# Half blocks, cast blocks and quarter stores of a two-level Winograd matmul on other queues and slots

## The chip, the cores and the metric

The kernel runs on one core of one Trainium2 chip. The metric is device time in microseconds (us) of one execution. Before the change it is 1529.64 us, the median of three runs (1527.75 to 1530.28). TensorE, VectorE, ScalarE and GpSimd work as separate engines; SyncE only issues transfers. In the lines of the profile they are PE (its weight loads PEld), DVE, ACT, POOL and SP. Transfers are issued by GpSimd (queue q0 of the page) and by SyncE (q1), and all of them run on the core's 16 DMA engines.

## The reference

```python
def setup_inputs():
    m, k, n = 4096, 4096, 4096
    return {"a": randn(m, k), "b": randn(k, n), "bias": randn(n)}   # float32

def reference(a, b, bias):
    return np.tanh(np.matmul(a, b) + bias)
```

## The kernel before

**Tiling.** The output is cut into four columns of 1024 (`c` = 0 to 3) and sixteen pairs of row blocks (256 rows). Of each pair and column the product is made by Winograd's variant of Strassen's scheme: the 256 x 4096 by 4096 x 1024 product is split into quadrants, and seven products of 16 matmuls of 128x128 by 128x512 (`m1` to `m7`, the table `PRODUCTS`) take the place of eight. Operands are fp16, sums float32. On the left stand the quadrants `a11`, `a12`, `a21`, `a22` and their sums `s1`, `s2`, `s5`, `s6`, `s7`; on the right `b11`, `b22` and the sums `d1`, `d3`, `d4`, `e6`, `e7`, each kept in four blocks (`b11_0` to `b11_3`). `b11_0` and `e6_0` are the two halves of one tile that is called `side`.

**Two pairs at once.** In columns 1, 2 and 3 most row pairs are taken by two (`fours`), and then most products are split a second time by the same scheme (`group0`, `group1`, `single`; 128x256 matmuls of line 764). For that `m2` and `m6` need forms of their right operand: quarters and the sums `t1`, `t2`, `t4`, `t3`. They are written to DRAM ahead of time by `put_four` and `put_sum`, and read back through a ring of five tiles (`b11_1`, `b11_2`, `b11_3`, `e6_2`, `e6_3`) by `pull_four`, each time that `let_go` frees one. So the blocks of `b11` and `e6` are overwritten while a column's fours run. Two halves that no form in DRAM holds are saved by `put_corner` and those of `m3`, `m4`, `m5` and `m7` that `t3` takes the place of are saved by `move(..., True)`.

**Leaving.** The last four of columns 1 and 2 (`leave` in `four`) must put the single blocks back, because the next row pairs use them whole. `give_back(c, step)` does that by the table `BACK`: `bring_block` reads a block back as two half blocks of 256 KB, `move(..., False)` returns the saved `t3` halves, `fetch` reads quadrants (`guest`), `load_nat` reads rows of `a` that must still be transposed, `load_raw` loads blocks of the next column's `b`. Steps 0 to 10 lie in the products of the four, 11 to 17 in the whole products `m1`, `m6`, `m7` at its end, 18 on in the slots behind. In the kernel before, `bring_block` uses GpSimd's queue at steps below `DIRECT` = 8 and SyncE's from there on; `move` always uses SyncE's. SyncE's queue carries the output stores, the quadrants and the writes of transposed rows too; each queue issues in program order, so a transfer that waits holds up those behind it.

**The leaving of column 1** ends with row pair 4; the next are pair 3 (item 25, its quadrants in DRAM already) and pair 2 (item 26), 0 and 1 (items 27, 28), whose rows are read in float32 and transposed by VectorE (`load_nat`, `turn`; line 237 for item 26, line 245 for 27 and 28). The second half of the four's last product `m7` is made between the first products of item 25. The rows of item 26 come at step 11 and just behind step 14; then, slot by slot (a slot is one product, 3.45 us), rows of 27 and 28 and blocks of column 2's `b` (`change`): `b12`, `b21`, then `b11`, `b22`, of which `bsum` makes `d3`, `e6`, `d1`, `d4`, `e7` on VectorE.

**Casting.** GpSimd's queue reads float32 blocks of `b` as four quarters of 128 KB, converted on the way. `cast_b` writes such a block of column 3 to DRAM in fp16, a quarter at each call, and `load_b` then reads it in one transfer. Before, this is done in the inner fours of column 2 (steps 0, 2, 6 and 9), for three whole blocks.

**Entering.** `begin_four` places the writes of forms around the start of the fours, in slots relative to `s0`, two items ahead: `ADDED` for `t3`, `STAGED` for `t1`, `t2`, `t4` (made on VectorE, so GpSimd's queue waits for it), `ASIDE` for the quarters, `SAVED` for the corners. From slot 8 on, `turn_over` carries out these slots itself (`slot(8)` and so on).

Of the kernel before, what the change touches and what calls it, by code (L numbers as in the profile page):

```python
# [44 lines left out]
SLOTS = 7  # L45
# [14 lines left out]
TWICE = (1, 2, 3)  # L60
# [3 lines left out]


FOUR = ((0, 0), "t1", (1, 0), "t2", "t3", (1, 1), "t4")
ADDED = {
# [3 lines left out]
}  # L71
STAGED = {1: (-8, -6, -4, 1, 4, 7), 2: (-8, -6, -4, 1, 4, 7), 3: (-8, -6, -4, 1, 4, 7)}
ASIDE = {1: (-7, -5, -3, 1, 3, 6), 2: (-7, -5, -3, 1, 3, 6), 3: (-12, -7, -10, -2, 6, 4)}
SAVED = {1: (-3, -2, 0, 2), 2: (-3, -2, 0, 2)}
SPARED = (0, 1)
S6_AT = 2
AWAY = {"m5": -14, "m7": -3}
# [7 lines left out]

CAST = [(3, blk, *half) for half in ((0, 1), (1, 0)) for blk in range(2)]
CASTING = {2: (0, 2, 6, 9)}


BACK = {
    1: {
        ("e6", 0): 6, ("e6", 1): 7, ("m7", "t3"): 7, ("guest", "a21"): 8, ("b11", 0): 9, ("b11", 1): 9, ("b11", 2): 10,
        ("b11", 3): 10, ("m5", "t3"): 9, ("m3", "t3"): 14, ("m4", "t3"): 15, ("nat", 1): 11, ("guest", "a12"): 10,
    },
# [4 lines left out]
    },  # L101
}
DIRECT = 8

OVER_FOUR = {"t3": (0, 1)}
HALF = (ds(0, NB // 2), ds(NB // 2, NB // 2))
# [14 lines left out]
def kernel(  # L121
# [7 lines left out]
    nc = tc.nc  # L129
# [53 lines left out]
    partner, begins, ends_with, firsts = {}, {}, {}, {}  # L183
# [33 lines left out]
    nat, aset = {}, {}  # L217
# [79 lines left out]
    def fetch(n, name, queue=nc.sync):  # L297
        for here, there in stored(n, name):
            queue.dma_start(out=here, in_=there)
# [53 lines left out]
    def cast_b(c, blk, h, j):  # L353

        to = dram.tile([P, TB, NB], fp16, name=f"cast_{c}_{blk}_{h}_{j}")
        for i in range(4):
            load_b(to, c, blk, h, j, quarters=(i,))
            if i == 3:
                cast[c, blk, h, j] = to
            yield  # L360
# [229 lines left out]
    def quarter(what, r, j, i):  # L590

        return bop[TWO[what][1], 2 * r + i][:, :, HALF[j]]
# [23 lines left out]
    def move(what, c, out_, *names):  # L616

        for name, (r, j) in OVER_FOUR.items():
            if names and name not in names:
                continue  # L620
            if out_:
                away[what, c, name] = dram.tile([P, TP, NB // 2], fp16, name=f"away_{what}_{c}_{name}")
            for i in range(2):
                there = away[what, c, name][:, ds(i * TB, TB)]
                here = quarter(what, r, j, i)
                nc.sync.dma_start(*(there, here) if out_ else (here, there))

    def twice_after(n, what):
        c, (pair,), part, _ = items[n]
# [53 lines left out]
    def bring_block(name, blk, queue=nc.gpsimd):  # L683
        what = {"b11": "m2", "e6": "m6"}[name]
        r, i = divmod(blk, 2)
        to = new_bop(name, blk)
        for j in range(2):
            there = corners[name, blk] if (r, j) == (0, 1) else forms[what, (r, j)][:, ds(i * TB, TB)]
            queue.dma_start(out=to[:, :, HALF[j]], in_=there)
# [162 lines left out]
    def give_back(c, step):  # L852
        for (name, part), at in BACK[c].items():
            if at == step:
                if name == "nat":
                    load_nat(ends_with[c] + 1, part)
                elif name == "guest":
                    fetch(ends_with[c], part)
                elif name in TWO:
                    move(name, c, False, part)  # L860
                elif name in ("b12", "b21"):
                    load_raw(name, c + 1, part, nc.sync)
                else:
                    bring_block(name, part, nc.gpsimd if step < DIRECT else nc.sync)

    left_over = []

    def four(n):
        c = items[n][0]
        p, q, m = n, n + 1, n + 2  # L870
        first, last = n == begins[c], m == len(items)
# [8 lines left out]
        def step(k):  # L880
            if leave:
                give_back(c, k)
            elif not first and not last and k in CASTING.get(c, ()):
                next(casts, None)

        def one_whole(what, i, steps=range(T)):
            _, left_, right = next(v for v in PRODUCTS.values() if v[0] == what)
# [221 lines left out]
        if last:  # L1109
# [15 lines left out]
            for what, (name, at, op, scale, r) in ends.items():  # L1125
                o, here = st[q][name], bank(q, 0, at)
# [44 lines left out]
    def begin_four(c):  # L1171
        s0 = SLOTS * (begins[c] - 2)
        n = next(n for n in firsts if firsts[n] == c)
        at_slot(SLOTS * n + 4, take_d, n)
        added = ADDED.get(c, {})
        for stage, slots in added.items():
            for add, at in enumerate(slots):
                at_slot(s0 + at, put_sum, *stage, add)
        for at, stage in zip(
            STAGED[c] + ASIDE[c],  # L1180
            [i for i in STAGES if i not in added] + [(w, f) for w in ("m2", "m6") for f in ((0, 0), (1, 0), (1, 1))],
        ):
            at_slot(s0 + at, put_four, *stage)
        for at, (name, blk) in zip(SAVED.get(c, ()), (("b11", 0), ("b11", 1), ("e6", 0), ("e6", 1))):
            at_slot(s0 + at, put_corner, name, blk)

    def turn_over(c):

        m = begins[c]
        p, q = m - 2, m - 1  # L1190
        left_count[0] = 0
        del free[:]

        def slot(at):
            for f, args in work.pop(SLOTS * p + at, ()):
                if f in (put_four, put_sum, put_corner):
                    f(*args)

        queue.extend(
            (what, f) for n in range(m, ends_with[c], 2) for what in ("m2", "m6")  # L1200
            for f in (FOUR if what == "m2" else (*FOUR[:5], *reversed(FOUR[5:])))
            if what == "m2" or n + 2 in fours or c == NC - 1
        )
        returned.clear()
        if c < NC - 1:
            returned.append(c)
        free.extend(("b11_1", "b11_2", "b11_3"))
        for i in range(3):
            pull_four()
        asum(q, "s1")  # L1210
        asum(q, "s6")
        fetch(m, "a11")
        slot(8)
        product(p, *PRODUCTS[8])
        single(p, "m4", 7)
        adds["m4"][1]()
        product(q, *PRODUCTS[2])
        resident_at(-7)
        single(p, "m4", 3)
        twice_after(p, "m4")  # L1220
        twice_four(p, "m4", 3)
        fetch(m, "a22")
        fetch(m + 1, "a22")
        fetch(m + 1, "a11")
        asum(q, "s7")
        slot(9)
        slot(10)
        seed(m, "d", 0)
        resident_at(-6)
        product(q, *PRODUCTS[5])  # L1230
        fetch(m, "a21")
        slot(12)
        resident_at(-5)
        slot(13)
        product(p, *PRODUCTS[10])
        resident_at(-4)
        seed(m, "w", 0)
        seed(m + 1, "w", 0)
        left(m, "m4", "v1")
        left(m, "m3", "v1")  # L1240
        slot(15)
        resident_at(-3)
        product(q, *PRODUCTS[8])
        fetch(m + 1, "a21")
        free.extend(("e6_2", "e6_3"))
        for i in range(2):
            pull_four()
        slot(17)
        resident_at(-2)
        seed(m, "c", 0)  # L1250
        product(q, *PRODUCTS[10])
        resident_at(-1)
# [50 lines left out]
    def at_slot(slot, f, *args):  # L1303
        work.setdefault(slot, []).append((f, args))
# [173 lines left out]
    first = new_sum([P, 4, 4, TB * QP], fp16, "first")  # L1478
    coarse = [bops.tile([P, 4, TB * QP], fp32, name="coarse", tag=t) for t in ("d3_1", "d3_2")]

    def load_first(m, queue, out_):
# [9 lines left out]
        out=ident, in_=ident, compare_op=mybir.AluOpType.is_equal, fill=0.0,  # L1491
# [146 lines left out]
    for c in TWICE:  # L1638
        s0 = SLOTS * next(n for n in range(len(items)) if items[n][0] == c)
        at_slot(s0 + 10, rights.clear)  # L1640
        at_slot(s0 + 10, new_right, "m4", "t1", "t2")
        if c == 2:
            at_slot(s0 + 10, new_right, "m4", "t4")
        at_slot(s0 + 10, new_right, "m3", "t1", "t2")
        at_slot(s0 + 12, new_right, "m3", "t4")
        if c != 2:
            at_slot(s0 + 14, new_right, "m4", "t4")
        for name, m3_at, m4_at in zip(("t1", "t2", "t4", "t3"), *FORMED):
            at_slot(s0 + m3_at, kept_form, "m3", name)
            at_slot(s0 + m4_at, kept_form, "m4", name)  # L1650
        at_slot(s0 + 14, new_lefts)
        if c < NC - 1:
            for what, there in (("m3", 6), ("m4", 10)):
                at_slot(s0 + there, move, what, c, True)
    for c in FOURS:
        begin_four(c)
    casts = (None for where in CAST for _ in cast_b(*where))
    groups = {}
    for n in partner:
        s0 = SLOTS * n  # L1660
# [15 lines left out]
    for slot in range(1 - len(ORDER), SLOTS * len(items)):  # L1676
        if slot in handed:
            if slot - 1 not in handed:
                c = max(c for c in FOURS if SLOTS * (begins[c] - 2) < slot)
# [50 lines left out]
```

## Time and the profile before

| What | before |
|---|---|
| median of three runs | 1529.64 us |
| the profiled execution | 1528.55 us |
| its span, first to last instruction | 1526.8 us |
| mean granted TensorE clock | 0.994 |
| bytes moved by DMA | 407.75 MB |
| transfers issued by GpSimd, share of 16 engines (q0) | 57.5% |
| transfers issued by SyncE (q1) | 36.6% |

Stretches are given in us from the span's start. In the table by stretches each engine has its busy time and in brackets its instructions; then come the granted TensorE clock (1.00 is full speed), the share of time that the packets of both queues together took on the 16 DMA engines (above 1 when packets of the two queues lie over each other), and GB/s. A line of the timeline has the start, the duration, the engine, the source line, the operation and its tiles, with the idle time of the engine before it and what ended it in square brackets. A line of an SP or POOL transfer there is its issue; when it landed is told by the table of DMA issues, whose last column is the median time from issue to landing.

### The profile page before, as it was taken

The numbers are of one execution on the slowest core, as the hardware profiler recorded it, in microseconds if no ns is written. First come the engines' busy times: TensorE is split into PE (matmuls) and PEld (weight loads), VectorE is DVE, ScalarE is ACT, GpSimd is POOL, SyncE is SP. The second block draws the span as 40 slices with busy tenths as digits, with TensorE's granted clock in tenths as the row PEclk, the third lists the DMA queues.
The fourth block names the chain that finished last, engine by engine and source line by source line (L and its number), as shares of the span: only waits on it lengthen the run. The fifth ranks groups of instructions, "written<-read, shape, count | busy, mean of one in ns | idle before, by whom it ended". The sixth has DMA issues, their size and how long they took to land.

```text
span 1526.8 us, 24983 instructions
## 1 busy us (share of the span) xinstructions
PE 1501.6 (98%) x9461; PEld 925.4 (61%) x9461; DVE 1214.9 (80%) x1718; ACT 403.4 (26%) x909; POOL 505.0 (33%) x894
## 2 busy tenths in 40 slices
PE   9999999999999999988999999999999999999998
PEld 4444444444445788853444578778744458888887
DVE  6788977777878888856788788789638869888888
ACT  4431111111222233320122223332212222333332
POOL 7765453433433111153553312222135121111112
PEclk9999999999999999998999999999999999999999
DMA  9999999999989788999997979999999687888895
GB/s 178 182 249 267 294 248 249 214 212 243 178 242 300 270 304 322 340 277 249 233 211 239 306 261 312 334 334 320 307 262 223 219 257 275 308 300 315 319 343 188
DMA packets 220269, 407.75 MB, mean 267 GB/s; under 512 B 25971, under 2 KB 114547, under 8 KB 220149
## 3 DMA queue, kind: packets, MB, share of 16 engines
q0 software_dynamic: 122320, 211.08, 57.5%
q1 hardware_dynamic: 97156, 194.68, 36.6%
q8 instruction: 74, 1.21, 0.3%
q10 hardware_dynamic: 672, 0.39, 0.1%
q14 instruction: 47, 0.38, 0.1%
HBM read 347.08 MB, written 133.69 MB: 315 GB/s over the span
## 4 chain that ended last, share of the span: by engine, by line
PE 86%; DMA 9%; DVE 2%; POOL 1%; issue 1%; SPq 0%; ACT 0%; DVEq 0%; POOLq 0%; ACTq 0%
PE ps L472 39%; PE ps L764 35%; PE ps L828 8%; PE ps L1414 4%; DMA nat<-in_a_dram 3%; DMA b<-in_b_dram 1%; DMA out_dram<-o 1%; DMA b<-form_m 1%; DMA out_dram<-ds 1%; DMA side<-in_b_dram 1%; DVE a L265 1%; DMA land<-in_a_dram 0%; POOL nat L228 0%; POOL land L1455 0%; DVE s L151 0%
## 5 line engine op out<-in xcount | busy, mean ns | idle before, releaser
L472 PEld LDWEIGHTS <-a 128*128 128x128 f16 x2592 | 254.0, 98 | 323.7 <-DMA b<-form_m 11.7
L764 PEld LDWEIGHTS <-h 128*128 128x128 f16 x2944 | 287.7, 98 | 37.4 <-DVE h L151 1.4
L700 POOL DMA_DIRECT2D form<-form_m x196 | 103.7, 530 | 551.6 <-PE ps L764 489.6
L764 PEld LDWEIGHTS <-a 128*128 128x128 f16 x2208 | 216.0, 98 | 36.2 <-issue 3.3
L472 PE MATMUL ps<-b,a 128*128 128x512 f16 x868 | 200.6, 382 | 11.6 <-DMA b<-form_m 10.3
L472 PE MATMUL ps<-d,a 128*128 128x512 f16 x800 | 182.2, 381 | 4.7 <-DVE ps L151 4.7
L265 DVE STREAM_TRANSPOSE a<-nat 128x1024 f16<-128x1024 f16 (+3 forms) x178 | 155.9, 918 | 18.4 <-PE ps L472 13.1
L375 POOL DMA_DIRECT2D b<-in_b_dram x240 | 129.5, 545 | 96.8 <-DMA b<-in_b_dram 30.1
L472 PE MATMUL ps<-e,a 128*128 128x512 f16 x700 | 159.2, 379 | 0.0
L151 DVE TENSOR_TENSOR a<-a,a 128x2048 f16<-128x2048 f16 (+1 forms) x123 | 148.2, 1205 | 0.2
L764 PE MATMUL ps<-form,h 128*128 128x256 f16 x1136 | 144.8, 273 | 0.1
L151 DVE TENSOR_TENSOR h<-a,h 128x1024 f16<-128x1024 f16 x184 | 125.1, 686 | 16.0 <-PE ps L764 15.6
L472 PEld LDWEIGHTS <-s 128*128 128x128 f16 x688 | 67.3, 98 | 79.9
L472 PE MATMUL ps<-d,s 128*128 128x512 f16 x496 | 112.1, 379 | 0.0
L764 PE MATMUL ps<-form,a 128*128 128x256 f16 x896 | 111.5, 273 | 0.2
L828 PE MATMUL ps<-d,a 128*128 128x512 f16 x480 | 108.2, 379 | 0.0
L237 POOL DMA_DIRECT2D nat<-in_a_dram x144 | 76.3, 534 | 87.5 <-DMA nat<-in_a_dram 42.2
L850 ACT CAST ps<-zeros 128x256 f32<-128x256 f16 x192 | 68.7, 380 | 133.7 <-DVE s L151 69.9
L828 PEld LDWEIGHTS <-a 128*128 128x128 f16 x608 | 59.8, 98 | 67.3 <-issue 2.2
L151 DVE TENSOR_TENSOR ds<-ds,ps 128x512 f32<-128x512 f32 (+1 forms) x126 | 83.5, 674 | 9.2 <-PE ps L828 8.3
L497 ACT ACTIVATE o<-ps 128x512 f32<-128x512 f32 x78 | 46.8, 600 | 122.0 <-issue 74.0
L151 DVE TENSOR_TENSOR ps<-ps,x 128x256 f32<-128x256 f32 x96 | 41.2, 430 | 45.0 <-PE ps L764 36.6
(160 smaller groups left out, 1938.6 us busy)
## 6 DMA issues: line engine op xcount, KB each, us to landing
form<-form_m POOLq DMA_DIRECT2D x196, 512.0 KB, 7.2
a<-scratch SPq DMA_DIRECT2D x147, 512.0 KB, 7.2
out_dram<-o SPq DMA_DIRECT2D x186, 256.0 KB, 6.0
nat<-in_a_dram POOLq DMA_DIRECT2D x256, 128.0 KB, 7.0
b<-in_b_dram POOLq DMA_DIRECT2D x208, 128.0 KB, 6.1
scratch<-a SPq DMA_DIRECT2D x48, 512.0 KB, 7.2
form_m<-stage POOLq DMA_DIRECT2D x18, 512.0 KB, 6.7
scratch<-a SPq DMA_DIRECT2D x32, 256.0 KB, 7.0
```

Of the source, the lines that this page charges most:

```text
L151: nc.vector.tensor_tensor(out=out_, in0=in0, in1=in1, op=op)
L237: nc.gpsimd.dma_start(out=tl[ds(q * QP, QP), :, :], in_=src.rearrange("(mb p) k -> p mb k", p=QP),)
L265: nc.vector.transpose(dst[:, ds(b0 * tb, n * tb), :].rearrange("P (b t) (mb p) -> P mb b t p", t=tb, p=QP), src[:, :, ds(b0, n), :].rearra ...
L375: nc.gpsimd.dma_start(out=dst[ds(q * QP, QP), ds(t, nt)], in_=src)
L472: nc.tensor.matmul(st[where], at, bt, start=(what == "m2" or n < LEAD and what == "m1") and i == 0, stop=i == len(ts_) - 1, skip_group_che ...
L497: nc.scalar.activation(o, src, TANH)
L700: nc.gpsimd.dma_start(out=rights[what, name], in_=forms[what, name])
L764: nc.tensor.matmul(to, at, bt, start=False, stop=t == TP - 1, skip_group_check=True)
L828: nc.tensor.matmul(to[:, half], at[:, t // TB, t % TB], bop[right, t // TB][:, t % TB, half], start=anew and t == 0, stop=t == T - 1, skip ...
L850: nc.scalar.copy(bank(n, 0, where)[:, HALF[half]], zeros)
L1414: nc.tensor.matmul(mb[m % 4, j], aq[m, kt // T][:, kt % T, :], right(kt, j), start=fresh and kt == k0, stop=stop and kt == k1 - 1, skip_gr ...
```

## The change

The halves that return when a four is left (`bring_block`, and `move` on its way back) all go through GpSimd's queue; the limit `DIRECT` is gone. In the table `BACK` all four blocks of `b11` and `m5`'s half come at step 10, `m7`'s half at 7, `m3`'s at 14 and `m4`'s at 15, in both columns; in column 1 the rows (`nat`) stay at step 11 and so stand behind the eight half blocks in that queue. Eight blocks of column 3 are cast in place of four (`CAST`: `b11` and `b22` of blocks 0 and 1 are new), through columns 1 and 2: at eight slots around each column's `turn_over`, in the first four at steps 0, 1, 2 and 9, in the inner ones at 2 and 9. Where a block is cast, one transfer of 512 KB takes the place of four quarters. In columns 1 and 2 the quarters of `m2` are written six slots earlier, its `t3` seven and eight earlier (as in column 3 before), the corners of `b11` four and three slots earlier and those of `e6` eight later.

```diff
-ADDED = {
-    1: {("m2", "t3"): (-5, -2), ("m6", "t3"): (2, 5)},
-    2: {("m2", "t3"): (-5, -2), ("m6", "t3"): (2, 5)},
-    3: {("m2", "t3"): (-12, -10), ("m6", "t3"): (2, 5)},
-}
...
-ASIDE = {1: (-7, -5, -3, 1, 3, 6), 2: (-7, -5, -3, 1, 3, 6), 3: (-12, -7, -10, -2, 6, 4)}
-SAVED = {1: (-3, -2, 0, 2), 2: (-3, -2, 0, 2)}
+ADDED = {c: {("m2", "t3"): (-12, -10), ("m6", "t3"): (2, 5)} for c in TWICE}
...
+ASIDE = {1: (-13, -11, -9, 1, 3, 6), 2: (-13, -11, -9, 1, 3, 6), 3: (-12, -7, -10, -2, 6, 4)}
+SAVED = {1: (-7, -5, 8, 10), 2: (-7, -5, 8, 10)}
...
-CAST = [(3, blk, *half) for half in ((0, 1), (1, 0)) for blk in range(2)]
-CASTING = {2: (0, 2, 6, 9)}
+CAST = [(3, blk, *half) for half in ((0, 1), (1, 0), (0, 0), (1, 1)) for blk in range(2)]
+CASTING = {1: (-12, -12, -11, -11, 12, 13, 15, 17), 2: (-12, -12, -11, -11, 12, 13, 15, 17)}
+CASTING_AT = {"first": (0, 1, 2, 9), "middle": (2, 9)}
...
 BACK = {
     1: {
-        ("e6", 0): 6, ("e6", 1): 7, ("m7", "t3"): 7, ("guest", "a21"): 8, ("b11", 0): 9, ("b11", 1): 9, ("b11", 2): 10,
-        ("b11", 3): 10, ("m5", "t3"): 9, ("m3", "t3"): 14, ("m4", "t3"): 15, ("nat", 1): 11, ("guest", "a12"): 10,
+        ("e6", 0): 6, ("e6", 1): 7, ("m7", "t3"): 7, ("b11", 0): 10, ("b11", 1): 10, ("b11", 2): 10, ("b11", 3): 10,
+        ("m5", "t3"): 10, ("m3", "t3"): 14, ("m4", "t3"): 15,
+        ("guest", "a21"): 8, ("guest", "a12"): 10, ("nat", 1): 11,
     },
     2: {
-        ("e6", 0): 6, ("e6", 1): 7, ("m7", "t3"): 8, ("m5", "t3"): 11, ("b11", 0): 9, ("b11", 1): 10,
-        ("m3", "t3"): 16, ("b11", 2): 17, ("b11", 3): 17, ("m4", "t3"): 15,
+        ("e6", 0): 6, ("e6", 1): 7, ("m7", "t3"): 7, ("b11", 0): 10, ("b11", 1): 10, ("b11", 2): 10, ("b11", 3): 10,
+        ("m5", "t3"): 10, ("m3", "t3"): 14, ("m4", "t3"): 15,
         ("b12", 0): 18, ("b12", 1): 18, ("b21", 0): 19, ("b21", 1): 19,
     },
 }
-DIRECT = 8
...
-                nc.sync.dma_start(*(there, here) if out_ else (here, there))
+                if out_:
+                    nc.sync.dma_start(out=there, in_=here)
+                else:
+                    nc.gpsimd.dma_start(out=here, in_=there)
...
-                    bring_block(name, part, nc.gpsimd if step < DIRECT else nc.sync)
+                    bring_block(name, part)
...
-            elif not first and not last and k in CASTING.get(c, ()):
-                next(casts, None)
+            elif not last and k in CASTING_AT["first" if first else "middle"]:
+                cast_on()
...
+    def cast_on():
+        next(casts, None)
+
     for c in FOURS:
         begin_four(c)
-    casts = (None for where in CAST for _ in cast_b(*where))
+        for at in CASTING.get(c, ()):
+            at_slot(SLOTS * (begins[c] - 2) + at, cast_on)
```

More of the change, by code (lines that the diff above doesn't have):

```diff
@@ L66 @@
 FOUR = ((0, 0), "t1", (1, 0), "t2", "t3", (1, 1), "t4")
-ADDED = {
[3 rows of a table removed]
-}
-STAGED = {1: (-8, -6, -4, 1, 4, 7), 2: (-8, -6, -4, 1, 4, 7), 3: (-8, -6, -4, 1, 4, 7)}
-ASIDE = {1: (-7, -5, -3, 1, 3, 6), 2: (-7, -5, -3, 1, 3, 6), 3: (-12, -7, -10, -2, 6, 4)}
-SAVED = {1: (-3, -2, 0, 2), 2: (-3, -2, 0, 2)}
+ADDED = {c: {("m2", "t3"): (-12, -10), ("m6", "t3"): (2, 5)} for c in TWICE}
+STAGED = {c: (-8, -6, -4, 1, 4, 7) for c in TWICE}
+ASIDE = {1: (-13, -11, -9, 1, 3, 6), 2: (-13, -11, -9, 1, 3, 6), 3: (-12, -7, -10, -2, 6, 4)}
+SAVED = {1: (-7, -5, 8, 10), 2: (-7, -5, 8, 10)}
 SPARED = (0, 1)
@@ L1195, in slot @@
             for f, args in work.pop(SLOTS * p + at, ()):
-                if f in (put_four, put_sum, put_corner):
+                if f in (put_four, put_sum, put_corner, cast_on):
                     f(*args)
@@ L1654 @@
                 at_slot(s0 + there, move, what, c, True)
+    casts = (None for where in CAST for _ in cast_b(*where))
+    def cast_on():
+        next(casts, None)
     for c in FOURS:
         begin_four(c)
-    casts = (None for where in CAST for _ in cast_b(*where))
+        for at in CASTING.get(c, ()):
+            at_slot(SLOTS * (begins[c] - 2) + at, cast_on)
     groups = {}
```

## The prediction

> **What bounds the kernel now.** I read the head of the page first, then the table by stretches for the places where PE isn't full, then timelines of PE, SP, POOL and DVE there.
>
> ```profile
> span 1526.8 us, 24983 instructions
> PE 1501.6 (98%) x9461; PEld 925.4 (61%) x9461; DVE 1214.9 (80%) x1718; ACT 403.4 (26%) x909; POOL 505.0 (33%) x894
> ```
> ```profile
> 680.00:700.00 20.00, 9.68 (x28) 3.21 (x26) 4.79 (x6) 0.63 (x1) 10.41 (x20) 0.66 1.15 251
> ...
> 1140.00:1160.00 20.00, 16.21 (x69) 6.92 (x68) 16.39 (x18) 5.53 (x10) 13.29 (x26) 0.91 1.16 190
> ```
>
> PE is the bound, so only its idle and slow time can be won: 1526.8 - 1501.6 = 25.2 us idle. 10.3 of it lie at 680 to 700, where column 1's fours are left, 3.8 at 1140 to 1160, where column 3 begins. The clock column adds something: 0.66 and 0.91. The PE timelines of both places show what that costs.
>
> ```profile
> 679.25 1.03 PE L472 MATMUL ps<-side,a 128*128 128x512 f16 x4
> ...
> 686.11 1.89 PE L472 MATMUL ps<-b,a 128*128 128x512 f16 x4 [4.97 <-DMA b<-form_m]
> 693.34 1.89 PE L472 MATMUL ps<-b,a 128*128 128x512 f16 x4 [5.34 <-DMA b<-form_m]
> 695.02 3.62 PE L828 MATMUL ps<-e,a 128*128 128x512 f16 x8
> ...
> 703.92 3.62 PE L472 MATMUL ps<-d,a 128*128 128x512 f16 x16
> 707.37 3.62 PE L472 MATMUL ps<-d,s 128*128 128x512 f16 x16
> ```
> ```profile
> 1134.29 1.03 PE L472 MATMUL ps<-e,s 128*128 128x512 f16 x4
> 1135.87 3.63 PE L472 MATMUL ps<-b,a 128*128 128x512 f16 x16 [0.55 <-DMA a<-scratch]
> ...
> 1146.74 5.01 PE L472 MATMUL ps<-d,a 128*128 128x512 f16 x16 [3.79 <-DVE ps L151]
> 1151.59 3.62 PE L472 MATMUL ps<-d,s 128*128 128x512 f16 x16
> ```
>
> Sixteen matmuls take 3.45 us (703.92 to 707.37). Item 25's `m2` begins at 679.25; `m2`, `m5` and the two halves of the old `m7` are three times 3.45, so `m3` could begin at 689.6. It begins at 703.9: **14.3 us** lost, 10.3 waiting for blocks 2 and 3 of `b11` and 4.0 at half clock (eight matmuls of line 828 take 3.4 in place of 1.7). In the second place four matmuls take 0.86, so `m5` could begin at 1135.15 and the third product behind it at 1145.5; it begins at 1151.6: **6.1 us**.
>
> Why the first wait: the chain of waits and the DMA issues of 669.3 to 675.
>
> ```profile
> 674.93 18.37 DMA b<-form_m
> ```
> ```profile
> b<-form_m SPq DMA_DIRECT2D x4, 256.0 KB, 18.4
> nat<-in_a_dram POOLq DMA_DIRECT2D x5, 128.0 KB, 9.0
> ```
>
> The halves sit in SP's queue while POOL's is full of rows, and take twice as long as these. Why the second: VectorE, by its timeline, waits for the last float32 quarter of `b22_0` before it makes `d3_0`, and the sums that PE needs stand behind it.
>
> ```profile
> 1141.45 1.23 DVE L151 TENSOR_TENSOR d<-b,b 128x2048 f16<-128x2048 f16 x1 [7.05 <-DMA b<-in_b_dram]
> ```
>
> **The change, part by part.** *The halves on POOL.* POOL's timeline at the leaving:
>
> ```profile
> 654.08 1.52 POOL L689 DMA_DIRECT2D e<-form_m  x2
> 661.48 1.51 POOL L689 DMA_DIRECT2D e<-form_m  x2 [5.88 <-PE ps L764]
> 666.53 0.55 POOL L299 DMA_DIRECT2D a<-scratch  x1 [3.55 <-PE ps L828]
> 667.07 3.74 POOL L237 DMA_DIRECT2D nat<-in_a_dram  x7
> 673.69 0.54 POOL L237 DMA_DIRECT2D nat<-in_a_dram  x1 [2.88 <-DMA a<-scratch]
> ```
> ```profile
> L237 POOL DMA_DIRECT2D nat<-in_a_dram x16: 532/536/577, 667.1 to 681.2; - x16
> ```
>
> A half costs 0.76 us of issue. Eight transfers are in flight at most: seven rows follow the quadrant at once, the eighth waits until that has landed, 6.9 us after its issue. Sixteen rows go out in 14.7 us, 0.92 each, so the k-th transfer from 661.48 on lands at 668.4 + 0.92(k-1). The new order is two of `e6`, eight of `b11` (k = 3 to 10), two of `m5`, `a11` (13), eight rows (to 21), two of `m3`, eight rows, two of `m4` (33).
> - `b11` is complete at 676.7; PE wants its last block at 681.8. The 14.3 us go. Its cover is 5 us.
> - The rows of item 26 come second. Their first eight land by 686.8, where before they were done before PE was. VectorE turns them ahead of the `m5` eviction that `m3` needs:
>
> ```profile
> 696.55 2.36 DVE L265 STREAM_TRANSPOSE a<-nat 128x1024 f16<-128x1024 f16 x2
> 698.83 1.18 DVE L151 TENSOR_TENSOR s<-a,a 128x2048 f16<-128x2048 f16 x1
> 702.39 0.70 DVE L151 TENSOR_TENSOR ps<-ps,s 128x512 f32<-128x512 f32 x1 [2.38 <-PE ps L472]
> ```
>
>   One transpose, the sum and the eviction are 3.1, so they must be there by 686.5: 0.3 late.
> - `m3`'s halves land at 688.6 (wanted 689.6), `m4`'s at 697.8 (wanted from 696.5, the second block 0.9 later): 0.4 late. At the pace of the issues, 0.76, nothing is late; at 1.0 the last half lands at 700.4, 3 late. I charge 1.
>
> What is late next is everything that POOL issues behind: rows of items 27 and 28 and column 2's `b`. PE and VectorE come 14 us earlier, and DMA was working through PE's pause.
>
> ```profile
> 695.00:700.00 5.00, 5.00 (x15) 1.90 (x14) 4.66 (x5) 0.00 (x0) 2.14 (x4) 0.60 1.17 251
> 705.00:710.00 5.00, 5.00 (x25) 2.29 (x24) 5.00 (x9) 1.60 (x3) 4.28 (x8) 1.00 0.93 187
> 720.00:725.00 5.00, 5.00 (x25) 2.25 (x23) 3.60 (x6) 0.60 (x1) 3.35 (x7) 1.00 0.70 204
> ```
> ```profile
> 721.65 4.28 POOL L245 DMA_DIRECT2D nat<-in_a_dram  x8 [11.64 <-PE ps L472]
> ...
> 759.59 0.54 POOL L375 DMA_DIRECT2D b<-in_b_dram  x1 [0.15 <-issue]
> ```
> ```profile
> b<-in_b_dram POOLq DMA_DIRECT2D x1, 128.0 KB, 11.1
> ```
> ```profile
> 772.09 1.22 DVE L151 TENSOR_TENSOR d<-b,b 128x2048 f16<-128x2048 f16 x1
> 773.23 1.28 DVE L151 TENSOR_TENSOR ps<-ps,s 128x512 f32<-128x512 f32 x2
> ```
> ```profile
> 776.44 3.62 PE L472 MATMUL ps<-d,a 128*128 128x512 f16 x16
> ```
>
> The tightest consumer is `d3_1` at 772.09: its last quarter (issued 759.59, the third fence tells its landing) is there at 770.7, 1.4 us ahead, and the eviction behind it has 1.9 before PE's 776.44. That is 3.3 us of cover against 13.3 (14.3 less the 1). The rest must come from POOL being earlier. By the formula the last half is issued at 690.5; sixteen rows follow until 705.2, eight until 712.6, and the last eight, which waited 11.64 us for PE, until 720; the `b` quarters follow 6.3 earlier than before. 13.3 - 6.3 - 3.3 = 3.7 us of stall. But SP's queue has lost sixteen half blocks, so POOL's pace should be nearer to 0.76, by which nothing is late. I take 3, between 0 and 3.7 plus 1.4 for a cold clock (the extra of 1146.74's sixteen).
>
> The Trainium skill, "DMA: Bandwidth & Descriptors", section "Issuing engines are not separate DMA queues", says that transfers of every issuing engine share the same sixteen DMA engines, so a queue change makes no capacity. The share of 1.17 agrees, and by this rule the first rival below would hold.
>
> *Column 2's leaving* moves the same halves, with no rows behind; POOL is idle there until 1114: nothing.
>
> *Eight cast blocks.* `b11` and `b22` of blocks 0 and 1 and the fourth early cast come as five transfers in place of twenty quarters. A cast block took longest at this place:
>
> ```profile
> b<-cast SPq DMA_DIRECT2D x3, 512.0 KB, 14.2
> ```
>
> Even so `b22_0`, issued when `m5` has let go of it at 1118, lands at 1132, 9 us before 1141.45. The 6.1 us go. The price is twenty more quarters written in columns 1 and 2. Sixteen stand around the starts, where POOL waits for VectorE or has nothing else; in the fours they share DMA with forms and stores. Before, the fours with casts lost two small pieces of PE time, 0.56 and 0.25 us; column 1 had 0.25 without. I charge 0.5, between 0 (more traffic wins nothing) and 2.
>
> *Quarter stores and corners* move out of 440 to 460 (share 1.08) into 400 to 440 (0.89 and 0.57):
>
> ```profile
> 400.00:420.00 20.00, 20.00 (x94) 9.11 (x93) 18.56 (x22) 5.18 (x9) 4.31 (x8) 1.00 0.89 208
> 420.00:440.00 20.00, 20.00 (x95) 9.00 (x94) 17.32 (x21) 4.57 (x8) 5.61 (x8) 1.00 0.57 174
> ```
>
> PE is full in both, so there is nothing to win but the 0.5 to 0.7 us lost at 462 and 846; I count none. If a moved store held POOL up, forms would be late; POOL waited 18.5 us for VectorE there, which is the cover.
>
> **Sum.** -14.3 + 1 + 3 - 6.1 + 0.5 = -15.9. The profiled execution took 1528.55 (1.75 beside its span), so 1512.6; the median is 1.1 above it: **1514** us.
>
> **Rivals.** *The backlog is handed on.* From 660 to 770 the DMA engines are the bound; PE's pause was what they needed, and it comes back at `d3_1`. For it: shares above 1.1 through the stretch. Against: 0.70 and 0.93 at 705 to 725, and POOL's 11.64 us of waiting for PE. At 1.04 a transfer (thirty-two quarters from 726.8 to 760.1) POOL is no earlier, and 13.3 - 3.3 + 1.4 = 11.4, with the 1 of the halves 12.4 of the 14.3, are lost: 1529.6 - 1.9 - 5.6 = 1522.
>
> *GpSimd's queue becomes the bound*, and it is slower. Place: 661 to 720. A half takes not 7 but 12 us to land, as the `b` quarters did at 1121 (the chain of waits has 13.79), so the pace is 1.5. `m4`'s halves then land at 661.5 + 12 + 48 = 721.5, 25 us after they are wanted, and with 4 us of cold clock 29 are lost for 14.3 won: 1529.6 + 14.7 - 5.6 = 1539. It decides from 10 us a landing (5 landings to the last half, 16 us late). Against: the same queue at the same place landed its rows in 9.0 while SP's was full, and kept a pace of 0.92.
>
> ```profile
> 1120.93 13.79 DMA b<-in_b_dram
> ```
>
> The Trainium skill, "SBUF — State Buffer", section "SBUF: two separate sides", has a cause: GpSimd writes descriptors through a port that some VectorE operations lock. The 0.76 us halves at 654, beside a full VectorE, speak against it.
>
> *Only one of the two works*: the casts, or the halves, fail to arrive in time; with the second alone it is 1524.
>
> **How the numbers follow.** Forecast 0.58 (1508 to 1518), backlog 0.20 (1518 to 1524.5), one part alone 0.08 (1520 to 1526), GpSimd bound 0.14. The low end is both losses and the two small pieces gone: 1529.6 - 20.4 - 1.2 = 1508. The range 1508 to 1525 leaves out the slower case and a part of the third. Runs agree within some 0.2% (3 us). Faster 0.84, same 0.03, slower 0.13 (some of the last two cases ends within 0.2%).
>
> **What would show it.** Right: no wait for `b<-form_m` at the leaving and a full clock; rows of line 237 issued some 10 us later; no VectorE wait for `b` before column 3. Wrong: PE waiting for `d<-away_m_t`, VectorE for `nat`, or `d3_1` of column 2 for `b`, by more than 5 us; or new PE idle time in column 1's fours.

## The result and the profile after

| kernel | median us | lowest to highest | runs | ratio to before, 95% interval |
|---|---|---|---|---|
| before | 1527.75 | 1524.99 to 1530.28 | 5 | |
| after | 1518.65 | 1517.44 to 1521.58 | 5 | 0.9945 (0.9925 to 0.9964) |

The change wins 9.1 us (1527.75 - 1518.65) where 15.6 were forecast. The profiled execution of after took 1521.58 us, the longest of its five, and so does not show the last 3 us of this. The head of its page:

```profile
span 1519.8 us, 24963 instructions
...
PE 1500.8 (99%) x9461; PEld 927.0 (61%) x9461; DVE 1214.8 (80%) x1718; ACT 403.1 (27%) x909; POOL 532.2 (35%) x930
```

PE issues the same 9461 matmuls in the same order and is as long busy as before (1500.8 against 1501.6). What fell is idle time: 1519.8 - 1500.8 = 19.0 us are left of 25.2. The table by stretches of after says where they lie (columns as in the prediction: busy time of PE, PEld, DVE, ACT, POOL, then clock, DMA share, GB/s):

```profile
680.00:700.00 20.00, 17.59 (x75) 7.53 (x73) 12.82 (x18) 2.34 (x4) 12.48 (x22) 0.91 1.07 237
700.00:720.00 20.00, 19.20 (x90) 8.62 (x89) 16.74 (x20) 1.68 (x3) 9.51 (x18) 1.00 1.15 272
760.00:780.00 20.00, 14.05 (x54) 5.74 (x53) 8.79 (x9) 3.07 (x6) 14.56 (x27) 0.83 1.18 174
1100.00:1120.00 20.00, 17.67 (x83) 7.87 (x82) 8.21 (x11) 2.12 (x4) 3.87 (x6) 1.00 1.04 367
1140.00:1160.00 20.00, 20.00 (x94) 9.09 (x93) 16.73 (x21) 6.64 (x12) 13.87 (x25) 1.00 1.15 205
```

680 to 700, which held 10.3 us of idle time, holds 2.4, and 1140 to 1160, which held 3.8, holds none. But 760 to 780, where PE had been full, now lacks 6.0 at a clock of 0.83, and 1100 to 1120 lacks 2.3. PE's timeline at the four places:

```profile
684.65 3.62 PE L469 MATMUL ps<-b,a 128*128 128x512 f16 x16
688.10 1.89 PE L828 MATMUL ps<-e,a 128*128 128x512 f16 x8
692.40 5.30 PE L469 MATMUL ps<-d,a 128*128 128x512 f16 x16 [2.41 <-DVE ps L148]
697.53 3.62 PE L469 MATMUL ps<-d,s 128*128 128x512 f16 x16
...
773.68 6.08 PE L469 MATMUL ps<-d,a 128*128 128x512 f16 x16 [5.95 <-DVE ps L148]
779.60 2.75 PE L469 MATMUL ps<-d,s 128*128 128x512 f16 x12
...
1110.88 1.04 PE L469 MATMUL ps<-side,a 128*128 128x512 f16 x4 [2.33 <-DMA a<-scratch]
...
1141.97 3.62 PE L469 MATMUL ps<-d,a 128*128 128x512 f16 x16
1145.43 3.62 PE L469 MATMUL ps<-d,s 128*128 128x512 f16 x16
```

The order of PE's work is the same, so the same matmul can be set side by side in both traces:

| matmul | before | after | difference |
|---|---|---|---|
| last product before column 1's fours are left | 659.26 | 659.58 | +0.3 |
| item 26, `m3`'s first sixteen | 703.92 | 692.40 | -11.5 |
| the next sixteen | 707.37 | 697.53 | -9.8 |
| column 2's first product behind `d3` | 776.44 | 773.68 | -2.8 |
| column 3, third product | 1146.74 | 1141.97 | -4.8 |
| the next sixteen | 1151.59 | 1145.43 | -6.2 |
| span | 1526.8 | 1519.8 | -7.0 |

Read downwards: the wait at the leaving is gone. Of the 14 us that it gave, the stall before 692.40 takes 2.41 and its half clock 1.7 (697.53 - 692.40 = 5.13, in place of 3.45), a gap of 0.80 follows at 712.31, and at 773.68 PE stands still for 5.95 and loses 2.5 to the half clock (779.60 - 773.68 = 5.92). Together 13.3: **column 1 gives back nearly all that it won**. What is left at the end is column 3's entry and some pieces of half a microsecond.

VectorE's timeline names the two causes in column 1:

```profile
686.48 1.25 DVE L262 STREAM_TRANSPOSE a<-nat 128x1024 f16<-128x1024 f16 x1 [2.00 <-DMA nat<-in_a_dram]
689.38 1.25 DVE L262 STREAM_TRANSPOSE a<-nat 128x1024 f16<-128x1024 f16 x1 [1.65 <-DMA nat<-in_a_dram]
690.55 1.18 DVE L148 TENSOR_TENSOR s<-a,a 128x2048 f16<-128x2048 f16 x1
691.65 0.69 DVE L148 TENSOR_TENSOR ps<-ps,s 128x512 f32<-128x512 f32 x1
...
768.38 1.23 DVE L148 TENSOR_TENSOR d<-b,b 128x2048 f16<-128x2048 f16 x1 [8.49 <-DMA b<-in_b_dram]
...
772.93 1.29 DVE L148 TENSOR_TENSOR ps<-ps,s 128x512 f32<-128x512 f32 x2
```

The eviction that `m3` needs (691.65) stands behind transposes that wait for rows of `A`. The eviction that column 2 needs (772.93) stands behind `d3_0`, which waits 8.49 us for the last quarter of `b22_0`. GpSimd's queue shows why that quarter is not earlier; first before, then after:

```profile
726.82 0.54 POOL L375 DMA_DIRECT2D b<-in_b_dram  x1 [0.90 <-issue]
...
732.80 1.58 POOL L375 DMA_DIRECT2D b<-in_b_dram  x3 [0.45 <-DVE a L265]
...
755.94 0.55 POOL L375 DMA_DIRECT2D b<-in_b_dram  x1 [1.46 <-DMA side<-in_b_dram]
```
```profile
662.63 1.49 POOL L689 DMA_DIRECT2D e<-form_m  x2 [4.82 <-PE ps L764]
...
683.17 0.53 POOL L234 DMA_DIRECT2D nat<-in_a_dram  x1 [1.33 <-DMA a<-scratch]
...
726.05 0.54 POOL L372 DMA_DIRECT2D b<-in_b_dram  x1 [0.95 <-DMA nat<-in_a_dram]
...
736.05 0.53 POOL L372 DMA_DIRECT2D b<-in_b_dram  x1 [1.09 <-DMA b<-in_b_dram]
...
750.77 0.56 POOL L372 DMA_DIRECT2D side<-in_b_dram  x1
...
760.64 1.61 POOL L372 DMA_DIRECT2D b<-in_b_dram  x3 [2.13 <-DMA side<-in_b_dram]
```

From 662.63 to the last of item 26's first eight rows at 683.17 it issues 21 transfers, one in 1.03 us (20.5 / 20). Before, it had waited 11.64 us for PE at 721; now its longest wait from 662.63 to 726.05 is 2.24 us, and still it reaches column 2's first quarter only 0.8 us earlier, while PE comes some 9 us earlier (9.8 by the table, less the gap of 0.80 at 712). From there it falls behind. The first eight quarters (`b12`) went out in 6.0 us before (726.82 to 732.80) and take 10.0 after (726.05 to 736.05), each held up by a row that has still to land. The last quarter of `b22_0` was issued at 755.94 before; after, it is the third of the three from 760.64, at about 761.7. So the transfer that `d3_0` waits for goes out 5.8 us later than before, not earlier.

### The profile page after: what moved, and what is told of

The parts are those of the page before. It is cut to its first block, busy times and chain, and to the rows that moved or that the text cites. A ratio compares the mean times of both kernels' runs of the same rounds, so it can differ in the third digit from the quotient of the medians.

```text
span 1519.8 us, 24963 instructions
## 1 busy us (share of the span) xinstructions
PE 1500.8 (99%) x9461; PEld 927.0 (61%) x9461; DVE 1214.8 (80%) x1718; ACT 403.1 (27%) x909; POOL 532.2 (35%) x930
## 4 chain that ended last, share of the span: by engine, by line
PE 89%; DMA 8%; POOL 1%; issue 1%; DVE 1%; ACT 0%; SPq 0%; DVEq 0%; POOLq 0%; ACTq 0%
PE ps L469 39%; PE ps L764 37%; PE ps L828 7%; PE ps L1414 5%; DMA nat<-in_a_dram 4%; DMA d<-away_m_t 1%; DMA b<-in_b_dram 1%; DMA a<-scratch 1%; DMA b<-corner_b 1%; DMA side<-in_b_dram 1%; POOL nat L234 0%; POOL nat L225 0%; DVE a L262 0%; DMA coarse<-in_a_dram 0%; POOL b L372 0%
## 5 line engine op out<-in xcount | busy, mean ns | idle before, releaser
L469 PEld LDWEIGHTS <-a 128*128 128x128 f16 x2592 | 254.5, 98 | 321.2 <-issue 18.8
L262 DVE STREAM_TRANSPOSE a<-nat 128x1024 f16<-128x1024 f16 (+3 forms) x178 | 156.2, 919 | 25.2 <-PE ps L469 13.1
L372 POOL DMA_DIRECT2D b<-in_b_dram x224 | 120.8, 545 | 92.3 <-PE ps L469 31.8
```

The costliest lines, as they stand in the source:

```text
L262: nc.vector.transpose(dst[:, ds(b0 * tb, n * tb), :].rearrange("P (b t) (mb p) -> P mb b t p", t=tb, p=QP), src[:, :, ds(b0, n), :].rearra ...
L372: nc.gpsimd.dma_start(out=dst[ds(q * QP, QP), ds(t, nt)], in_=src)
L469: nc.tensor.matmul(st[where], at, bt, start=(what == "m2" or n < LEAD and what == "m1") and i == 0, stop=i == len(ts_) - 1, skip_group_che ...
```

## The experiments

Each kernel ran on a chip together with the kernel before; the ratios are to that. Kernels that ran together share a chip: the first four in the table ran beside a before of 1532.65 us, the next four with 1527.97, the next three with 1529.80, the last with 1529.45.

| kernel | median us | ratio, 95% interval |
|---|---|---|
| returns alone | 1519.62 | 0.9920 (0.9905 to 0.9935) |
| casts and slots alone | 1523.56 | 0.9945 (0.9931 to 0.9960) |
| after, `b21` behind `b22` | 1516.60 | 0.9904 (0.9885 to 0.9922) |
| after, `b21` in 128 KB | 1512.53 | 0.9875 (0.9855 to 0.9895) |
| after, again | 1518.43 | 0.9938 (0.9917 to 0.9959) |
| returns alone, again | 1521.53 | 0.9949 (0.9930 to 0.9968) |
| returns alone, `b21` in 128 KB | 1515.19 | 0.9914 (0.9890 to 0.9938) |
| after, 128 KB, two blocks later | 1515.00 | 0.9911 (0.9884 to 0.9937) |
| before, `b21` in 128 KB | 1530.33 | 1.0002 (0.9988 to 1.0015) |
| after, 128 KB, `m5` on SP | 1513.39 | 0.9887 (0.9865 to 0.9908) |
| after, 128 KB, `b21` behind `b22` | 1511.79 | 0.9880 (0.9859 to 0.9902) |
| the last, without seven stores | 1514.16 | 0.9881 (0.9859 to 0.9903) |

### Each part alone

The returns alone undo the tables of slots and casts (`ADDED`, `ASIDE`, `SAVED`, `CAST`, `CASTING`):

```diff
-CASTING = {1: (-12, -12, -11, -11, 12, 13, 15, 17), 2: (-12, -12, -11, -11, 12, 13, 15, 17)}
+CASTING = {2: (0, 2, 6, 9)}
```

> The returns through GpSimd's queue alone; cast blocks, quarter stores and corners as before. Theory 1 (what the half blocks win at column 1's leaving is handed back by column 2's start, because the loads behind them in GpSimd's queue come no earlier): the wait for b<-form_m is gone, a wait of VectorE for column 2's b of 8 us or so is there, column 2's leaving loses 2.4, column 3's entry still waits: 1526 to 1529 us, the same as before (1527.75). By the forecast's own sum (14.3 less 4 kept at column 1): 1516 to 1519. Rival (the casts and the shifted slots cost column 1 the time, not the returns): 1514 to 1518, with no wait for b at column 2's first sums.

The casts alone undo `BACK`, `move` and `bring_block`:

```diff
-                    bring_block(name, part)
+                    bring_block(name, part, nc.gpsimd if step < DIRECT else nc.sync)
```

> Eight cast blocks, quarter stores and corners in the new slots; the returns as before. Theory 1: column 3's entry wins its 6.1, the small waits at 462, 659, 846 and 992 us go (0.5 each), the 10.3 us wait at 680 to 700 stays: 1519 to 1522 us, so nearly all of the change's gain. Rival (the casts' traffic takes away from column 1): 1523 to 1527.

The medians of these four are read against their own before (1532.65), which was 4.9 us slower than the 1527.75 that the expected times go by. The casts alone came close to what was expected, 6 to 9 us below before: they won 9.1, with both waits for `b<-form_m` in place and no wait for a sum at column 3, though PE waits there 2.31 us for a quadrant (`a<-scratch`, at 1134.49). The returns alone did not come as expected. They won 13.0 us, and column 3's entry, which was to wait as before, lost only 0.26. PE and VectorE of the returns alone there:

```profile
1137.55 3.62 PE L472 MATMUL ps<-e,s 128*128 128x512 f16 x16
1141.42 3.61 PE L472 MATMUL ps<-d,a 128*128 128x512 f16 x16 [0.26 <-DVE ps L151]
```
```profile
1136.13 1.23 DVE L151 TENSOR_TENSOR d<-b,b 128x2048 f16<-128x2048 f16 x1 [2.80 <-DMA b<-in_b_dram]
```

`d3_0` starts at 1136.13, not at 1141.45, with the same float32 quarters of `b22_0` to wait for. Before, `b11`'s last two blocks returned at the same time as these quarters, through SP's queue from 1113 on; now they are through by 1103, and the quarters land faster: the median from 1108 to 1140 falls from 11.2 to 4.9 us. So **either part alone takes column 3's wait away**, and together they can't take it twice. That it was these four half blocks, and not the other returns that came earlier, was not tried apart. That made a new question: do the casts, on top of the returns, add anything or cost something?

> The changed kernel once more, beside the same runs of before as the next three. Theory A (the casts and the returns win the same wait at column 3's entry, since either one frees a queue there, so the casts add nothing to the returns): ratio to before 0.992 to 0.993, equal to that of the returns alone. Theory B (the casts' traffic and the shifted slots cost what the returns win): ratio 0.9945, 2 us or more over the returns alone.

> The returns alone, once more, beside the changed kernel. Theory A: within 2 us of the changed kernel, either side, ratio 0.992. Theory B: 2 to 4 us below the changed kernel. In both, PE idles 4 to 6 us at column 2's first sums.

After was 0.9938 and the returns alone 0.9949, within each other's intervals: theory B, by which the casts cost 2 us or more, falls. The medians differ by 3.1 us in after's favour, more than theory A's 2, but the two samples overlap from 1517.3 to 1522.3, so what the casts add stays between nothing and some 3 us. What the returns add on top of the casts is as little (0.9945 against 0.9938 and 0.9945). The returns alone show the same new wait in column 1 as after; PE's waits in the second run:

```profile
PE ps L472 <- DVE ps L151: 8.0, 4, 5.3
```

That is 8.0 us in four waits, of which the 5.3 stands before column 2's first product behind `d3`. The casts are not its cause.

### GpSimd's queue at column 2's start

`d3_0` needs `b12` and `b22`. Between them the queue holds column 2's first two `b21` blocks, sixteen transfers of 64 KB. The first edit moves them behind, the second halves their number:

```diff
-            at_slot(s0 + (8 if part else -2), load_raw, "b21", c, blk)
+            at_slot(s0 + (8 if part else 4 if c == 2 else -2), load_raw, "b21", c, blk)
```

> The changed kernel, and column 2's first two b21 blocks (sixteen quarters of 64 KB) are loaded behind b11 and b22, not ahead of them. Theory 1 (GpSimd's queue order decides: VectorE's first sum d3_0 needs b12 and b22, which stand behind sixteen transfers that it doesn't need): VectorE's 8.5 us wait and PE's 5.95 us idle with its half clock at 774 go, 7 to 9 us: 1510 to 1512 against 1518.65. Rival (DMA is short of bandwidth through all of 690 to 770, so something is late in any order): the wait moves to d4 or e7, which need b21, and the time is 1517 to 1520.

```diff
-        nt = TB // 2 if c == 2 and name == "b21" else TB
+        nt = TB
```

> The changed kernel, and column 2's b21 is loaded in quarters of 128 KB: half as many transfers, the same bytes. If the number of transfers sets the pace (eight in flight, about 0.9 us each), eight fewer bring b22 some 7 us earlier and the wait at 774 nearly goes: 1511 to 1514. If bytes set it: no change, 1518 to 1520.

With `b21` behind, the wait at 774 is gone, but the time missed its mark of 1512: it is 3.0 us below the returns alone on the same chip (1519.62). VectorE and PE of the profiled execution (1522.78 us, the longest of its six):

```profile
816.61 1.29 DVE L148 TENSOR_TENSOR g<-d 128x1024 f16<-128x1024 f16 x2
831.65 1.29 DVE L148 TENSOR_TENSOR stage<-b,stage 128x1024 f16<-128x1024 f16 x2 [13.75 <-DMA form_m<-stage]
```
```profile
827.12 2.75 PE L469 MATMUL ps<-b,a 128*128 128x512 f16 x12
837.21 6.24 PE L469 MATMUL ps<-e,a 128*128 128x512 f16 x16 [7.33 <-DVE ps L148]
```

The wait moved, not to `d4` or `e7` as the rival had it, but 60 us on, to a staged form whose write stands behind the late quarters in the same queue. So in this execution order alone hands the backlog on. The execution took 6.2 us more than the median of the six, so how much is lost there in the others is not shown.

With 128 KB quarters it shrinks. GpSimd's timeline and PE's waits:

```profile
734.63 0.55 POOL L372 DMA_DIRECT2D b<-in_b_dram  x1 [1.09 <-DMA b<-in_b_dram]
...
744.05 2.14 POOL L372 DMA_DIRECT2D side<-in_b_dram  x4
```
```profile
PE ps L469 <- DVE ps L148: 5.0, 3, 2.4
```

Eight transfers take 9.4 us of the queue (734.63 to 744.05) where sixteen with the same bytes took 14.7 in after (736.05 to 750.77): 1.18 each against 0.92. In the other traces sixteen took 12.7 to 15.3 us and eight 7.8 to 9.4. Half the bytes saves about a fifth of a transfer's turn, so **the number counts more than the bytes**. The Trainium skill, "DMA: Bandwidth & Descriptors", section "Anatomy of one DMA — SWDGE (gpsimd) path", states a fixed part of about 2 us in each transfer, whatever its size; the two paces agree with a fixed part, but can't test its size, since several transfers overlap here. PE's longest wait fell from 5.95 to 2.40 and the time to 1512.53, inside the 1511 to 1514. In its profiled execution PE is 2.7 us ahead of after's already at the last product of the fours (656.84 against 659.58). Was that one run's early start the gain? The same edit on the returns alone, and on before:

> The returns alone, with column 2's b21 in quarters of 128 KB. Theory (eight transfers fewer ahead of b22 bring it 4 to 6 us earlier, whatever else is in the kernel): 5 to 8 us below the returns alone, that is a ratio of 0.987 to 0.989, with PE's idle time at column 2's first sums at 2.5 us or less and no half clock. Rival (the gain of 128 KB quarters came from that run's early start alone, 2.3 us): 2 us below or the same.

> The kernel before, with column 2's b21 in quarters of 128 KB, and nothing else. Theory (column 2's loads are late only where PE has not stood still for 10 us at column 1's leaving): no wait is there to be won, 0 to 1.5 us below before. Rival (fewer transfers help everywhere, by less contention): 3 us or more below.

On the returns alone it took 6.3 us on the same chip (1521.53 to 1515.19), inside the 5 to 8, though its ratio, 0.9914, is above the 0.987 to 0.989 that was expected; PE waits 0.99 us at column 2's first product behind `d3`, with no half clock behind it. On before it took nothing. Fewer transfers are worth only what is late, and in before nothing is late there. That fits the reading that the backlog is worked off during PE's pause at the leaving.

Both edits together:

> The changed kernel with 128 KB quarters for b21 and the first two b21 blocks behind b11 and b22. Theory: the wait at column 2's first sums (2.3 us of PE's time) is gone; the forms behind b21 in GpSimd's queue, which were 7.3 us late at 837 us with sixteen 64 KB quarters, are late by less, 0 to 3 us, since eight transfers fewer stand ahead: 0 to 3 us below the 128 KB quarters alone (ratio 0.985 to 0.988). Rival: 5 us or more are lost at 837 us as before: 0.990 to 0.992.

No wait is left at 768 nor at 837 (in PE's waits the longest is 2.5 us, at item 26). The ratio is 0.9880, the top of the range; against 0.9875 for the 128 KB quarters alone the order adds nothing that can be measured.

### The stall at item 26, and the queue or the engines

> The changed kernel with 128 KB quarters, and the two halves of m5 in column 1's leaving return through SP's queue. Theory (the stall of 2 to 3 us and its half clock at 692 is the rows of item 26 standing behind fourteen returned transfers, each about 1 us): the rows land 2 us earlier, the stall shrinks to about 0.5 and the half clock goes, 3 to 5 us below the 128 KB quarters alone (ratio 0.984 to 0.986), if none is taken back at column 2. Rival (the sixteen DMA engines set when the rows land, not the order in one queue): the rows land as before, no change, or m5's halves are late on SP and PE waits for b<-away_m_t, 2 to 5 us above.

```diff
-                    nc.gpsimd.dma_start(out=here, in_=there)
+                    (nc.sync if what == "m5" and c == 1 else nc.gpsimd).dma_start(out=here, in_=there)
```

Transfers at 662 to 684 (tile, queue, count, KB, median us to land): with `m5` on GpSimd's queue (128 KB quarters, `b21` behind), then with `m5` on SP's:

```profile
b<-form_m POOLq DMA_DIRECT2D x5, 256.0 KB, 8.6
nat<-in_a_dram POOLq DMA_DIRECT2D x8, 128.0 KB, 7.9
```
```profile
nat<-in_a_dram POOLq DMA_DIRECT2D x8, 128.0 KB, 10.3
b<-away_m_t SPq DMA_DIRECT2D x2, 256.0 KB, 12.6
a<-scratch SPq DMA_DIRECT2D x1, 512.0 KB, 18.8
```

The rows were issued 3.0 to 3.9 us earlier (0.9 of it because the whole queue began earlier) and took 2.4 us longer, SP's own transfers took 11 to 19 us where they had taken 7 to 10, and the stall stayed (2.43 at 692.10, 2.51 before the move), as did the time (0.9887). That is the rival: moving a transfer from one queue to another made no room here. The last kernel takes transfers away instead; it leaves those parts of the output unwritten:

```diff
+        if quiet:
+            return
         nc.sync.dma_start(
             out=out[ds((2 * pair + r) * P, P), ds(c * NCW + j * NB, NB)], in_=o
         )
```

> 128 KB quarters for b21 and the first two b21 blocks behind b22, and in column 1's leaving the results of items 24 and 25 are not stored (six or seven stores of 256 KB from 662 to 681 us are left out, so those parts of the output are not written). Theory (the transfers of both queues share the engines that carry them: what SP stores there stretches every landing of GpSimd's queue): a half block lands in 6.5 to 7.5 us, not 8.5; the eighth row of item 26 lands 2 to 4 us earlier against PE's last product before it, and the 2.5 us stall with its half clock at 692 goes or shrinks below 0.5: a ratio of 0.984 to 0.986. Rival (one queue's order and its eight in flight set the pace, whatever SP does): landings of 8 to 9 us, stall 2 to 3 us, 0.987 to 0.989.

The same view of it, and PE's timeline:

```profile
b<-form_m POOLq DMA_DIRECT2D x5, 256.0 KB, 7.5
nat<-in_a_dram POOLq DMA_DIRECT2D x9, 128.0 KB, 6.7
```
```profile
687.73 1.89 PE L832 MATMUL ps<-e,a 128*128 128x512 f16 x8
689.47 3.61 PE L469 MATMUL ps<-d,a 128*128 128x512 f16 x16
692.92 3.62 PE L469 MATMUL ps<-d,s 128*128 128x512 f16 x16
697.30 3.77 PE L469 MATMUL ps<-d,a 128*128 128x512 f16 x16 [0.77 <-DMA d<-away_m_t]
...
711.64 4.85 PE L469 MATMUL ps<-b,a 128*128 128x512 f16 x11 [3.66 <-DVE s L148]
```

Landings are about a microsecond shorter (7.5 against 8.6 for the forms, 6.7 against 7.9 for the rows) and `m3` starts at 689.47 with no stall, as the theory had it. But the time is unchanged (0.9881): 0.77 us are lost at 697 for `m4`'s half blocks and 3.66 at 711, with a half clock behind it. PE came 2.8 us earlier (689.47 against 692.28) and met the next late rows (VectorE waits 3.92 us for `nat` at 709.16). Besides the stores, SP's load of 512 KB left this stretch, since without stores ahead of it it was issued at 655 and not at 665; the shorter landings belong to both.

### Column 2's leaving

> The changed kernel with 128 KB quarters for column 2's b21, and in column 2's leaving the last two b11 blocks return at step 17 as before, not at step 10. If the six transfers that returned early crowd SP's loads of A at 1100 us: PE's wait for a<-scratch (2.3 us in the changed kernel, 1.5 with 128 KB quarters) goes, and the time is 1.5 to 2 us below the 128 KB quarters alone: a ratio of 0.986. If they come back as a new wait at column 3's entry (SP's or GpSimd's loads there are late): 0.988 to 0.990.

```diff
-    ... ("b11", 2): 10, ("b11", 3): 10,
+    ... ("b11", 2): 17, ("b11", 3): 17,
```

PE's wait for `a<-scratch` stayed (1.66 us; 1.53 with 128 KB quarters alone). The two early blocks are not its cause. The ratio, 0.9911, is above both expected ones, but its interval overlaps that of the 128 KB quarters alone. The view of transfers of after at 1095 to 1104 shows what is slow: SP's loads of `A` land in 11 us, beside GpSimd's half blocks. The same view has 4.4 us in before, 4.9 in the casts alone and 9.8 in the returns alone, where PE waits 1.31 us; so the returns bring this wait, not the casts.

```profile
a<-scratch SPq DMA_DIRECT2D x6, 256.0 KB, 11.0
d<-away_m_t POOLq DMA_DIRECT2D x4, 256.0 KB, 8.5
```

Which of the others would have to wait, so that these loads come in time, was not tried.

## Why the prediction was right in sign and off in size

- **The returned half blocks** (-14.3): right. No wait for `b<-form_m` is left, and the leaving is through 14 us earlier.
- **Rows behind the halves** (+1): mis-sized. It measured 4.9 (2.41 idle, 1.7 half clock, 0.80 at 712). The formula had item 26's first eight rows landed at 686.8; the second transpose had its rows at 689.4. The queue began 1.15 us later than the formula's 661.48, and the pace was 1.03, at the edge of the 1.0 that the prediction bounded `m3` and `m4` with; what it had not priced at that pace were the rows, and the half clock behind a gap of 2.4.
- **The backlog** (+3): **this step failed**. It measured 8.4 (5.95 idle, 2.5 half clock). "The `b` quarters follow 6.3 earlier than before" was the false link: the first came 0.8 earlier, and the last of `b22_0`, which `d3_0` needs, 5.8 later. The prediction let the pace fall towards 0.76, because SP's queue had lost sixteen half blocks. It did not fall: the sixty-five transfers from 662.63 to 726.05 went out at 0.98, the thirty-five steps from there to `b22_0`'s last quarter at 1.02, where before the same steps took 0.83. The transfers had only changed queues, and the run with `m5` on SP and the run without stores show that a landing is stretched by what the other queue carries.
- **The first rival** (the backlog is handed on, 1518 to 1524.5) had the mechanism and the place, column 2's `d3`, and the measured 1518.65 lies at the edge of its range, outside the forecast's 1508 to 1518. Its end, 1522, was 3.4 high, the forecast's 1514 was 4.7 low. That its sum came so near (12.4 us lost of 14.3, 13.3 measured) is in part luck: it put 1 on the halves and 11.4 on `d3`, where 4.9 and 8.4 were measured, and its pace before, 1.04, counts thirty-two quarters from 726.8 to 760.1 where the queue issued forty transfers (those of `b21` are two to a quarter), 0.83 each. It put the wait at `d3_1`; it came at `d3_0`, three operations earlier on VectorE, and `d3_1` behind it no longer waited. The rule of the Trainium skill that stood beside it ("DMA: Bandwidth & Descriptors", "Issuing engines are not separate DMA queues": a queue change makes no capacity) was to be taken as it stands: the traces agree with it (two half blocks moved to SP, 7.9 to 10.3 us a row; seven stores left out, 8.6 to 7.5 us a form).
- **The casts** (-6.1): size right (from -0.1 at 1110 to -6.2), its reading half right. The prediction took the float32 quarters for the cause. The returns alone, which keep them, lose the same wait, so the returns of before, beside these quarters, were as much a cause. The rival "only one of the two works" took the parts for independent and gave 1524 to the casts alone; the casts alone came out 9.1 below their before, the returns alone between 6.4 and 13.0, and both together 9.1 and 9.5.
- **Column 2's leaving** (nothing): wrong by 2.3. POOL was idle there, but SP was not, and its loads of `A` landed in 11.0 us and not in 4.4 beside the new transfers. Which of these would have to wait stays open.
- **Quarter stores** (none): 0.52 at 462 and 0.66 at 846 are gone, as is one of 0.56 at 992. The prediction had mentioned the first two and not counted them.
- **The second rival** (GpSimd as the bound, 1539) needed 10 us a landing; the half blocks landed in 8.5.

What would show it: no wait for `b<-form_m` held, and so did no VectorE wait for `b` before column 3:

```profile
1134.22 1.22 DVE L148 TENSOR_TENSOR d<-b,b 128x2048 f16<-128x2048 f16 x1
```

The rows of item 26 were issued 8.1 us later (675.13 for 667.07), near the 10. The full clock did not hold (0.91 at 680 to 700), and the sign of being wrong, a `d3` of column 2 waiting over 5 us for `b`, is there with 8.49.

## What to carry to other kernels

When PE pauses, ask what the DMA engines do in the meantime. If they were working through a backlog, closing the pause can move the wait to the next consumer; find that consumer and shorten the queue ahead of it before you count the gain, best by fewer transfers, since their number counted here more than their bytes, and a move to another queue won nothing. Two edits that cure the same wait by different ways do not add up, so a wait with two causes is counted once.

## What the runs showed of the hardware

- Splitting a 128 KB load into two of 64 KB on GpSimd's queue cost 0.66 us for each load (2 x 0.92 - 1.18), in a queue that stood full: sixteen took 14.7 us and eight 9.4.
- With two half blocks moved to SP's queue, a 512 KB load on SP landed in 18.8 us instead of 9.8, and the rows on GpSimd's in 10.3 instead of 7.9 (medians), at a stage where the DMA share is 1.05.
- A stop of PE for 2.4 us at 692 was followed by a half clock that cost 1.7 us. A stop as long at 767.80 in the changed kernel with 128 KB quarters cost no clock: sixteen matmuls behind it took 3.45 (767.80 to 771.25). The length alone does not decide: in the returns alone 2.21 us at 690.72 cost none, and with 128 KB quarters besides 1.98 us at 691.12 did.

```profile
767.80 3.61 PE L469 MATMUL ps<-d,a 128*128 128x512 f16 x16 [2.40 <-DVE ps L148]
771.25 3.62 PE L469 MATMUL ps<-d,s 128*128 128x512 f16 x16
```

What decides was not settled.
